# A hybrid attention layer in two-part fp32r: feature-major products as three 256-column matmuls into one shared bank

## The chip, the core and the metric

The kernel runs on one core of one Trainium2 chip. The metric is the device time of one execution in microseconds (us). The kernel before was run three times: 1160.6, 1161.08 and 1163.76 us, so its median is 1161.08 us. A profile of one further execution is what the argument is read from.

## The reference, cut to what matters

The input is 256 tokens of 2048 float32 features. One layer is computed:

```
h = rms_norm(x, attn_norm)
x = x + concat(norm(forgetting_attention), norm(stick_breaking_attention)) @ w_out   # both from h @ w_in
h = rms_norm(x, ffn_norm)
u = causal_conv3(h @ w_up) + conv_b          # depthwise, width 3 along the tokens, 11264 features
x = x + (silu(gate half of u) * value half of u) @ w_down                            # 5632 features
```

Everything is float32. Some 51 million weights are read once each; the profile counts 208.36 MB read from HBM.

## The kernel before, in words

**Two-part products.** TensorE's operands here are of the type fp32r, to which a float32 is rounded when it is written. To keep float32's accuracy, each operand a is split into `hi` = a rounded to fp32r and `lo` = a - `hi`, and a product sums three parts: hi·hi, hi·lo and lo·hi. `weights` (lines 202 to 215) brings 128 x 2048 weights (a piece: one DMA of 1024 KB into `w_raw`, three buffers), rounds them on ScalarE (ACT, line 210, `w_hi`, two buffers) and subtracts on VectorE (DVE, line 211, `w_lo`, two buffers). There are 204 such pieces. The activations are split once and stay: `hT[:, k]` is feature tile k, transposed, as [128 features, 2 parts, 256 tokens].

**Token-major products** (`token_major`, lines 220 to 240) hold 128 tokens of activations in the array (a load of 128 x 128, LDWEIGHTS) and stream 512 (in three column groups 344) columns of weights past them: three matmuls per feature tile and token tile, lines 235, 236 and 237, each with a load of its own. They serve most projections, the output projection and the down-projection.

**Feature-major products** (`feature_major`, lines 244 to 266) hold the weights in the array and stream the tokens, so that the result comes out as [features, tokens]. They serve the queries and keys of the stick-breaking attention (`sb_heads`, lines 474 to 483, eight calls) and the whole up-projection (`up_pair`, lines 599 to 606, 44 calls: 22 for gate tiles and 22 for value tiles). A call makes two tiles of 128 features from two pieces of weights. Per feature tile k and tile j of the two there are two matmuls: line 258 streams both parts of `hT[:, k]`, 512 columns, past `hi`, so that hi·hi lands in columns 0 to 255 of the tile's own PSUM bank and hi·lo in columns 256 to 511; line 262 streams 256 columns past `lo` and adds to the second half. With 16 feature tiles, 2 tiles j and 52 calls there are 1664 such pairs. The two halves of a bank are added afterwards: in `convolved` (lines 580 to 597) by an ACT copy of one half (line 586) and a DVE add (line 587), then a DVE product with the tokens' factor `R` (line 588), one ACT and two DVE operations of the convolution (lines 590 and 594), for each tile of 256 columns. `sb_heads` does the like in lines 480 to 482. The gate (lines 613 to 620) is a silu on ACT, a DVE product, and the split of the result into `g`, tile by tile.

**PSUM.** Eight banks: four of the pool `psa` (tag "acc"), and two each of the tags "s" and "t" of `psb`. A feature-major call takes two banks; in the up-projection every third call takes the two of tag "s".

**Order.** Every engine takes its instructions in one written order. The tile framework makes that order by priority; the weights' DMA, rounding and subtraction are given a priority 200 steps ahead of their place in the program (`AHEAD`), so that they stand between the convolution's instructions on ACT and DVE. The attention heads are generators, of which one step each is issued after a piece (`step`). The feed-forward runs in three parts of 16, 16 and 12 of the 44 gate tiles (`FFN_PARTS`): 32, 32 and 24 pieces of up-projection, each part followed by its share of the down-projection (16, 16 and 12 pieces).

Of the kernel before, what the change touches and what calls it, by code (L numbers as in the profile page):

```python
# [28 lines left out]

# Columns of the constant array.  # L30
C_ID, C_TRI, C_ONE = (P * i for i in range(3))
# [12 lines left out]
def hybrid_layer(  # L44
# [36 lines left out]

# [1 line left out]
    NC2 = 2 * NFT  # L83
# [48 lines left out]

# [1 line left out]
    pcol = const.tile([P, 50], F32, name="pcol")  # L134
# [12 lines left out]
    def transposed_split(k, g):  # L147
        """Feature tiles k and k + 1 of the tokens' rows, transposed, times g, in two parts."""
        ps = psb.tile([P, 2, S], F32, name="ps_x", tag="t")
        for j in range(2):  # L150
            for t in range(NT):
                nc.tensor.transpose(  # L152
                    ps[:, j, t * P : (t + 1) * P], xt[t][:, (k + j) * P : (k + j + 1) * P], ident
                )
        for j in range(2):
            i = k + j
            act.activation(hT[:, i, 0, :], ps[:, j, :], AF.Identity, scale=g[:, i : i + 1])
            dve.scalar_tensor_tensor(
                hT[:, i, 1, :], ps[:, j, :], g[:, i : i + 1], f32(hT[:, i, 0, :]),
                op0=ALU.mult, op1=ALU.subtract,  # L160
            )

    def sums_of_squares(ss, c):
        """Of 512 columns of each token tile."""
        for t in range(NT):
            junk = tmp.tile([P, 512], F32, name="junk", tag="raw", bufs=4)
            act.activation(junk, xt[t][:, c * 512 : (c + 1) * 512], AF.Square, accum_out=ss[:, t, c : c + 1])

    def token_factors(ss, n):
        """1 / rms of each token: per partition, and in every partition."""  # L170
        rstd = const.tile([P, NT], F32, name=f"rstd{n}")
        ssum = small.tile([P, NT], F32, name="ssum", tag="ssum")
        dve.tensor_reduce(ssum, ss, axis=AX.X, op=ALU.add)
        rsqrt(rstd, ssum, 1.0 / D, NT)
        dg = []
        for t in range(NT):
            dg.append(small.tile([P, P], F32, name="dg", tag="dg", bufs=2))
            dve.tensor_scalar(dg[t], ident, rstd[:, t : t + 1], None, op0=ALU.mult)
        return rstd, dg
# [8 lines left out]

# [1 line left out]
    waiting = deque()  # L190
# [9 lines left out]

# [1 line left out]
    def weights(src, a, b):  # L202
# [17 lines left out]
    def token_major(lhs, w, k0, nk, c0, cols, pieces=None, before=None):  # L220
        """[tokens, cols] = lhs.T @ w[k0:k0+nk, c0:c0+cols] for both token tiles."""
        acc = [psa.tile([P, 512], F32, name=f"acc{t}", tag="acc") for t in range(NT)]
# [21 lines left out]
    def feature_major(w, c0, spare):  # L244
        """Two tiles of features, each [features, tokens] in two summands."""
        nonlocal n_acc
        acc = []
        for j in range(2):
            pool, tag = (psa, "acc") if n_acc % 3 or not spare else (psb, "s")
            acc.append(pool.tile([P, 512], F32, name="pu", tag=tag))  # L250
        n_acc += 1
        for kh in range(2):
            hi, lo = weights(rows_of(w, 8 * kh, 8, c0, 2 * P), 8, 2 * P)
            for i in range(8):
                k = 8 * kh + i
                for j in range(2):
                    fs = slice(j * P, (j + 1) * P)
                    nc.tensor.matmul(  # L258
                        acc[j], hi[:, i, fs], hT[:, k].rearrange("p a b -> p (a b)"),
                        start=k == 0, stop=False,  # L260
                    )
                    nc.tensor.matmul(  # L262
                        acc[j][:, S:], lo[:, i, fs], hT[:, k, 0, :], start=False, stop=k == KT - 1
                    )
            step()
        return acc

    with ExitStack() as actx:
# [9 lines left out]
        def to_heads(dst, rows, t, scale):  # L278
            """Four heads' [tokens, dims] to [dims, tokens], times scale."""
            ps = psb.tile([P, 4, P], F32, name="ps_h", tag="t")  # L280
# [4 lines left out]
        def fox_rows(acc, dst, g):  # L285
            """Queries or keys of four heads: normalised, then transposed."""
            rows = []
# [19 lines left out]

        # The last four heads come when the projections are through with hT, and are used up
        # before its last rows are written again.
        oT = [at.tile([P, 2, S], F32R, name=f"oT{h}") for h in range(2 * NH - 4)]  # L310
# [3 lines left out]
        def attended(po, h, g, group):  # L314
            """Output of a head, [dims, tokens]: times its norm's weight in two parts, and its squares."""
            o = oT[group * NH + h]
# [10 lines left out]

# [1 line left out]
        # The first columns of weights are taken as x arrives.  # L329
        def opening(k, n):  # L330
# [52 lines left out]
        def gates():  # L383
            # log_sigmoid(y) = min(y, 0) - ln(1 + exp(-|y|))
            la = tmp.tile([P, NT, NH], F32, name="la", tag="la")
# [7 lines left out]
            yield  # L393
            # Cumulative log gates, the head h of row r*8+h, over the tokens.
            pc = psb.tile([P, 512], F32, name="pc", tag="t")
# [71 lines left out]

# [1 line left out]
        B0 = 3 * WF + NH  # L469
# [4 lines left out]
        def sb_heads(c0, scale, name):  # L474
            dst = heads_tile(name)
            for i in range(0, 4, 2):
                acc = feature_major(wi, c0 + i * P, False)
                for j in range(2):
                    t2 = tmp.tile([P, S], F32, name="t2", tag="t1", bufs=3)
                    act.copy(t2, acc[j][:, S:])  # L480
                    dve.tensor_tensor(t2, acc[j][:, :S], t2, op=ALU.add)
                    dve.tensor_tensor(dst[:, i + j, :], t2, scale, op=ALU.mult)
            return dst

        def sb_head(h, qT, kT, v):
# [8 lines left out]
            mm(z1, identR, maskS, start=False, stop=True)  # L494
            # softplus(z) = max(z, 0) + ln(1 + exp(-|z|))
            e = tmp.tile([P, 3 * P], F32, name="e", tag="pr")
# [8 lines left out]
            yield  # L505
            # z - sum of softplus over the keys from s on: the exponent of the weights.
            for i in range(2):
# [22 lines left out]

# [1 line left out]
        ss2 = const.tile([P, NT, 4], F32, name="ss2")  # L532
# [38 lines left out]

# [1 line left out]
    ff = ctx.enter_context(tc.tile_pool(name="ff", bufs=2))  # L573
    nu = 6
    up = [ff.tile([P, 2 + S], F32, name=f"up{i}") for i in range(nu)]
    for u in up:
        dve.memset(u[:, 0:2], 0.0)
    n_up = 0

    def convolved(ps, f):  # L580
        """Feature tile f after the up-projection, its token factor and its convolution."""
        nonlocal n_up
        u = up[n_up % nu]
        n_up += 1
        t2 = ff.tile([P, S], F32, name="t2", tag="t2", bufs=3)
        act.copy(t2, ps[:, S:])  # L586
        dve.tensor_tensor(t2, ps[:, :S], t2, op=ALU.add)  # L587
        dve.tensor_tensor(u[:, 2:], t2, R, op=ALU.mult)  # L588
        a = ff.tile([P, S], F32, name="cv", tag="cv", bufs=6)
        act.activation(  # L590
            a, u[:, 2:], AF.Identity, scale=ccol[:, 2, f : f + 1], bias=ccol[:, 3, f : f + 1]
        )
        for w in range(2):
            dve.scalar_tensor_tensor(  # L594
                a, u[:, w : w + S], ccol[:, w, f : f + 1], a, op0=ALU.mult, op1=ALU.add
            )
        return a

    def up_pair(f0):
        """Two feature tiles."""  # L600
        nonlocal R
        acc = feature_major(wu, f0 * P, True)
        if R is None:
            R = in_every_partition(dg2, 2)
            convolution_parameters()
        return [convolved(acc[j], f0 + j) for j in range(2)]

    gT = {}
    for n_part, (f_lo, f_hi) in enumerate(FFN_PARTS):
        for f in range(f_lo, f_hi, 2):  # L610
            gate = up_pair(f)
            val = up_pair(NFT + f)
            for j in range(2):
                sg = ff.tile([P, S], F32, name="sg", tag="sg")
                act.activation(sg, gate[j], AF.Silu)
                dve.tensor_tensor(sg, sg, val[j], op=ALU.mult)
                g2 = ff.tile([P, 2, S], F32R, name="g2", tag="g2", bufs=24)
                act.copy(g2[:, 0, :], sg)
                dve.tensor_tensor(g2[:, 1, :], sg, f32(g2[:, 0, :]), op=ALU.subtract)  # L619
                gT[f + j] = g2  # L620
        for c in range(4):
# [63 lines left out]
```

## Time and profile before

| | |
|---|---|
| three runs, median (lowest to highest) | 1161.08 us (1160.6 to 1163.76) |
| span of the profiled execution, first to last instruction | 1158.9 us |
| what lies around the span (median less span; the profile gives no other time of its own execution) | 2.2 us |
| TensorE matmul busy, records | 1147.0 us, 6002 |
| TensorE weight loads busy, records | 980.7 us, 6002 |
| DVE busy / ACT busy | 732.1 us (63%) / 559.1 us (48%) |
| DMA | 211.40 MB, mean 182 GB/s |

Times are counted from the first instruction of the execution. Engines: PE is TensorE's matmul, PEld its weight load, DVE VectorE, ACT ScalarE, SPq the queue that issues the DMAs. A line such as "L258 PE MATMUL pu<-hT,w_hi 128*128 128x512 f32 x1664 | 586.0, 397 | 0.0" reads: line 258 of the kernel, engine, operation, output from inputs, size of the loaded weights and of the result, number of instructions | busy time in us, mean ns of one | idle time of the engine just before them. Matmuls are pipelined, so a matmul's own duration overlaps with the next one's. A line of the timeline begins with the start and the duration in us.

### The profile page before, as it was taken

To read this page: it belongs to the slowest core of one execution; us is meant where nothing else is said; L and a number is where in the kernel's file an instruction comes from. 1 tells how busy PE (TensorE), PEld (TensorE's weight loads), DVE (VectorE), ACT (ScalarE), POOL (GpSimd) and SP (SyncE) were. 2 spreads that over 40 slices of the span, in tenths; PEclk is the share of its full clock that TensorE was granted. 3 is DMA by queue.
4 is the path that set the end of the run, shared out by engine and by line. 5 is a ranking of instruction groups with operands and counts; after the bars stand their busy time and mean duration, and the time that the engine had idled before them with its cause. 6 is when DMAs were issued, how large, how long until landed. Compare 5 with 4: busy or idle time off the path is not lost.

```text
span 1158.9 us, 14648 instructions
## 1 busy us (share of the span) xinstructions
PE 1147.0 (99%) x6002; PEld 980.7 (85%) x6002; DVE 732.1 (63%) x960; ACT 559.1 (48%) x716; POOL 0.2 (0%) x4
## 2 busy tenths in 40 slices
PE   7999999999999999999999999999999999999998
PEld 5998888888888888888888888888888888888886
DVE  4646656556465667777774547777775456777753
ACT  4644444445564555555553335555554334555531
POOL 0000000000000000000000000000000000000000
PEclk9999999999999999999999999999999999999999
DMA  6666545554444555555556555655556655555662
GB/s 226 212 219 204 179 149 181 158 171 150 159 158 151 182 170 194 182 182 183 183 189 199 191 182 183 196 194 190 182 185 198 197 183 182 183 188 184 192 231 76
DMA packets 162540, 211.40 MB, mean 182 GB/s; under 512 B 3736, under 2 KB 117546, under 8 KB 162474
## 3 DMA queue, kind: packets, MB, share of 16 engines
q1 hardware_dynamic: 162474, 210.47, 56.5%
q8 instruction: 47, 0.77, 0.3%
q14 instruction: 19, 0.16, 0.0%
HBM read 208.36 MB, written 2.10 MB: 182 GB/s over the span
## 4 chain that ended last, share of the span: by engine, by line
PE 97%; DVE 1%; ACT 1%; DMA 0%; issue 0%; SPq 0%
PE pu L258 33%; PE pu L262 17%; PE acc L235 14%; PE acc L237 14%; PE acc L236 14%; DVE w_lo L211 1%; ACT w_hi L210 1%; PE ps_x L152 1%; DMA x<-in_x_dram 0%; PE ps_h L282 0%; PE ps_z L491 0%; PE ps_s L423 0%; PE ps_o L517 0%; PE ps_o L450 0%; PE ps_p L444 0%
## 5 line engine op out<-in xcount | busy, mean ns | idle before, releaser
L211 DVE TENSOR_TENSOR w_lo<-w_raw,w_hi 128x2048 fp32r<-128x2048 f32 (+2 forms) x204 | 450.7, 2210 | 341.1 <-ACT w_hi L210 340.8
L258 PE MATMUL pu<-hT,w_hi 128*128 128x512 f32 x1664 | 586.0, 397 | 0.0
L210 ACT CAST w_hi<-w_raw 128x2048 fp32r<-128x2048 f32 (+2 forms) x204 | 375.7, 1842 | 368.1 <-PE acc L237 164.7
L262 PE MATMUL pu<-hT,w_lo 128*128 128x256 f32 x1664 | 466.6, 281 | 0.1
L258 PEld LDWEIGHTS pu<-hT,w_hi 128*128 128x128 f32 x1664 | 312.1, 188 | 73.7
L262 PEld LDWEIGHTS pu<-hT,w_lo 128*128 128x128 f32 x1664 | 314.3, 189 | 0.7 <-DVE w_lo L211 0.5
L237 PE MATMUL acc<-w_hi,g 128*128 128x512 f32 x352 | 139.0, 395 | 0.0
L235 PE MATMUL acc<-w_hi,g 128*128 128x512 f32 x352 | 138.9, 395 | 0.0
L236 PE MATMUL acc<-w_lo,g 128*128 128x512 f32 x352 | 138.9, 395 | 0.0
L235 PE MATMUL acc<-w_hi,hT 128*128 128x512 f32 (+1 forms) x320 | 119.8, 376 | 0.0
L236 PE MATMUL acc<-w_lo,hT 128*128 128x512 f32 (+1 forms) x320 | 119.1, 372 | 0.1
L237 PE MATMUL acc<-w_hi,hT 128*128 128x512 f32 (+1 forms) x320 | 118.9, 372 | 0.0
L594 DVE SCALAR_TENSOR_TENSOR cv<-up,ccol,cv 128x256 f32<-128x256 f32 x176 | 84.3, 479 | 1.6 <-ACT cv L590 0.7
L237 PEld LDWEIGHTS acc<-w_hi,g 128*128 128x128 f32 x352 | 66.3, 188 | 15.7 <-DVE g L619 0.2
L235 PEld LDWEIGHTS acc<-w_hi,g 128*128 128x128 f32 x352 | 66.3, 188 | 15.5
L236 PEld LDWEIGHTS acc<-w_lo,g 128*128 128x128 f32 x352 | 66.3, 188 | 15.4
L236 PEld LDWEIGHTS acc<-w_lo,hT 128*128 128x128 f32 x320 | 60.5, 189 | 9.0 <-DVE w_lo L211 0.9
L237 PEld LDWEIGHTS acc<-w_hi,hT 128*128 128x128 f32 x320 | 60.6, 189 | 8.7
L235 PEld LDWEIGHTS acc<-w_hi,hT 128*128 128x128 f32 x320 | 60.5, 190 | 8.2
L586 ACT COPY t<-pu 128x256 f32<-128x256 f32 x88 | 31.5, 360 | 58.8 <-PE pu L262 58.8
L590 ACT ACTIVATE cv<-up,ccol 128x256 f32<-128x256 f32 x88 | 52.6, 597 | 7.9 <-DVE up L588 5.6
L587 DVE TENSOR_TENSOR t<-pu,t 128x256 f32<-128x256 f32 x88 | 36.8, 420 | 21.9 <-ACT t L586 21.9
(148 smaller groups left out, 648.3 us busy)
## 6 DMA issues: line engine op xcount, KB each, us to landing
w_raw<-in_w_up_dram SPq DMA_DIRECT2D x88, 1024.0 KB, 5.1
w_raw<-in_w_down_dram SPq DMA_DIRECT2D x44, 1024.0 KB, 5.3
w_raw<-in_w_in_dram SPq DMA_DIRECT2D x36, 1024.0 KB, 5.2
w_raw<-in_w_out_dram SPq DMA_DIRECT2D x16, 1024.0 KB, 5.1
w_raw<-in_w_in_dram SPq DMA_DIRECT2D x12, 688.0 KB, 5.1
w_raw<-in_w_in_dram SPq DMA_DIRECT2D x8, 512.0 KB, 5.2
out_dram<-x SPq DMA_DIRECT2D x8, 256.0 KB, 5.3
x<-in_x_dram SPq DMA_DIRECT2D x3, 512.0 KB, 6.1
```

The lines of the kernel that those rows point to most:

```text
L152: nc.tensor.transpose(ps[:, j, t * P : (t + 1) * P], xt[t][:, (k + j) * P : (k + j + 1) * P], ident)
L210: act.copy(hi[:, :n], raw[:, :n])
L211: dve.tensor_tensor(lo[:, :n], raw[:, :n], f32(hi[:, :n]), op=ALU.subtract)
L235: nc.tensor.matmul(o, lhi, hi[:, i, :], start=first, stop=False)
L236: nc.tensor.matmul(o, lhi, lo[:, i, :], start=False, stop=False)
L237: nc.tensor.matmul(o, llo, hi[:, i, :], start=False, stop=last)
L258: nc.tensor.matmul(acc[j], hi[:, i, fs], hT[:, k].rearrange("p a b -> p (a b)"), start=k == 0, stop=False,)
L262: nc.tensor.matmul(acc[j][:, S:], lo[:, i, fs], hT[:, k, 0, :], start=False, stop=k == KT - 1)
L586: act.copy(t2, ps[:, S:])
L587: dve.tensor_tensor(t2, ps[:, :S], t2, op=ALU.add)
L590: act.activation(a, u[:, 2:], AF.Identity, scale=ccol[:, 2, f : f + 1], bias=ccol[:, 3, f : f + 1])
L594: dve.scalar_tensor_tensor(a, u[:, w : w + S], ccol[:, w, f : f + 1], a, op0=ALU.mult, op1=ALU.add)
```

## The change

`feature_major` now issues three matmuls of 256 columns each for a feature tile k and tile j: (`hi`, part 0), (`hi`, part 1) and (`lo`, part 0), all adding to the same 256 columns. The two tiles j share one bank, as the two halves of a [128, 2, 256] accumulator; only the very first matmul of the call clears. There are no two halves to be added any more, so the ACT copy and the DVE add go, and what follows works on both tiles at once: the product with `R` (or the scale of the queries and keys), the silu, the gate's product and its split run on 512 columns. The convolution's three operations stay per tile. The buffers are regrouped: four `up` buffers of two tiles for six of one, four `cv` of two for six of one, twelve `g2` of two tiles for 24 of one. The diff, without comments that it drops:

```diff
-        acc = []
-        for j in range(2):
-            pool, tag = (psa, "acc") if n_acc % 3 or not spare else (psb, "s")
-            acc.append(pool.tile([P, 512], F32, name="pu", tag=tag))
+        pool, tag = (psa, "acc") if n_acc % 3 or not spare else (psb, "s")
+        acc = pool.tile([P, 2, S], F32, name="pu", tag=tag)
...
-                    nc.tensor.matmul(
-                        acc[j], hi[:, i, fs], hT[:, k].rearrange("p a b -> p (a b)"),
-                        start=k == 0, stop=False,
-                    )
-                    nc.tensor.matmul(
-                        acc[j][:, S:], lo[:, i, fs], hT[:, k, 0, :], start=False, stop=k == KT - 1
-                    )
+                    for n, (a, b) in enumerate(((hi, 0), (hi, 1), (lo, 0))):
+                        nc.tensor.matmul(
+                            acc[:, j, :], a[:, i, fs], hT[:, k, b, :],
+                            start=k + j + n == 0, stop=k == KT - 1 and n == 2,
+                            skip_group_check=True,
+                        )
...
-                for j in range(2):
-                    t2 = tmp.tile([P, S], F32, name="t2", tag="t1", bufs=3)
-                    act.copy(t2, acc[j][:, S:])
-                    dve.tensor_tensor(t2, acc[j][:, :S], t2, op=ALU.add)
-                    dve.tensor_tensor(dst[:, i + j, :], t2, scale, op=ALU.mult)
+                dve.tensor_tensor(
+                    dst[:, i : i + 2, :], acc, scale.unsqueeze(1).to_broadcast([P, 2, S]), op=ALU.mult
+                )
...
-        t2 = ff.tile([P, S], F32, name="t2", tag="t2", bufs=3)
-        act.copy(t2, ps[:, S:])
-        dve.tensor_tensor(t2, ps[:, :S], t2, op=ALU.add)
-        dve.tensor_tensor(u[:, 2:], t2, R, op=ALU.mult)
-        a = ff.tile([P, S], F32, name="cv", tag="cv", bufs=6)
...
+        dve.tensor_tensor(u[:, :, 2:], ps, R.unsqueeze(1).to_broadcast([P, 2, S]), op=ALU.mult)
+        a = ff.tile([P, 2, S], F32, name="cv", tag="cv", bufs=4)
+        for j in range(2):
...
-            for j in range(2):
-                sg = ff.tile([P, S], F32, name="sg", tag="sg")
-                act.activation(sg, gate[j], AF.Silu)
-                dve.tensor_tensor(sg, sg, val[j], op=ALU.mult)
-                g2 = ff.tile([P, 2, S], F32R, name="g2", tag="g2", bufs=24)
-                act.copy(g2[:, 0, :], sg)
-                dve.tensor_tensor(g2[:, 1, :], sg, f32(g2[:, 0, :]), op=ALU.subtract)
-                gT[f + j] = g2
+            act.activation(gate, gate, AF.Silu)
+            dve.tensor_tensor(gate, gate, val, op=ALU.mult)
+            g2 = ff.tile([P, 2, 2, S], F32R, name="g2", tag="g2", bufs=12)
+            act.copy(g2[:, 0], gate)
+            dve.tensor_tensor(g2[:, 1], gate, f32(g2[:, 0]), op=ALU.subtract)
+            for j in range(2):
+                gT[f + j] = g2[:, :, j, :]
```

More of the change, by code (lines that the diff above doesn't have):

```diff
@@ L573, in hybrid_layer, with convolved @@
     ff = ctx.enter_context(tc.tile_pool(name="ff", bufs=2))
-    nu = 6
-    up = [ff.tile([P, 2 + S], F32, name=f"up{i}") for i in range(nu)]
+    nu = 4
+    up = [ff.tile([P, 2, 2 + S], F32, name=f"up{i}") for i in range(nu)]
     for u in up:
-        dve.memset(u[:, 0:2], 0.0)
+        dve.memset(u[:, :, 0:2], 0.0)
     n_up = 0
-    def convolved(ps, f):
+    def convolved(ps, f0):
         nonlocal n_up
@@ L584, in convolved @@
         n_up += 1
-        t2 = ff.tile([P, S], F32, name="t2", tag="t2", bufs=3)
-        act.copy(t2, ps[:, S:])
-        dve.tensor_tensor(t2, ps[:, :S], t2, op=ALU.add)
-        dve.tensor_tensor(u[:, 2:], t2, R, op=ALU.mult)
-        a = ff.tile([P, S], F32, name="cv", tag="cv", bufs=6)
[L590 to L595, printed above, removed]
-            )
+        dve.tensor_tensor(u[:, :, 2:], ps, R.unsqueeze(1).to_broadcast([P, 2, S]), op=ALU.mult)
+        a = ff.tile([P, 2, S], F32, name="cv", tag="cv", bufs=4)
+        for j in range(2):
+            f = f0 + j
+            act.activation(
+                a[:, j, :], u[:, j, 2:], AF.Identity,
+                scale=ccol[:, 2, f : f + 1], bias=ccol[:, 3, f : f + 1],
+            )
+            for w in range(2):
+                dve.scalar_tensor_tensor(
+                    a[:, j, :], u[:, j, w : w + S], ccol[:, w, f : f + 1], a[:, j, :],
+                    op0=ALU.mult, op1=ALU.add,
+                )
         return a
@@ L605, in up_pair @@
             convolution_parameters()
-        return [convolved(acc[j], f0 + j) for j in range(2)]
+        return convolved(acc, f0)
     gT = {}
```

## The prediction

> **What bounds the kernel now.** I read the page first, then the weight loads' waits, then the timeline of TensorE, which has what the page lacks: the time from one matmul's start to the next.
>
> ```profile
> span 1158.9 us, 14648 instructions
> PE 1147.0 (99%) x6002; PEld 980.7 (85%) x6002; DVE 732.1 (63%) x960; ACT 559.1 (48%) x716; POOL 0.2 (0%) x4
> PEclk9999999999999999999999999999999999999999
> PE 97%; DVE 1%; ACT 1%; DMA 0%; issue 0%; SPq 0%
> L258 PE MATMUL pu<-hT,w_hi 128*128 128x512 f32 x1664 | 586.0, 397 | 0.0
> L262 PE MATMUL pu<-hT,w_lo 128*128 128x256 f32 x1664 | 466.6, 281 | 0.1
> ```
> ```profile
> PEld pu L262 <- DVE w_lo L211: 0.5, 1, 0.5
> ```
>
> TensorE is the bound: 97% of the chain that ended last is its own work, at a granted clock that never falls. In the feature-major products it waits for nobody: 0.0 and 0.1 us idle before 3328 matmuls, and one wait of 0.5 us before a weight load. There is no stall to win back, so the change is worth what it does to TensorE's pace. The means of one (397 and 281 ns) aren't that pace, since neighbours overlap. The pace is the distance of the starts, first in the middle third of the up-projection, then in its first third:
>
> ```profile
> 699.67 0.39 PE L258 MATMUL pu<-hT,w_hi 128*128 128x512 f32 x1
> 699.90 0.28 PE L262 MATMUL pu<-hT,w_lo 128*128 128x256 f32 x1
> 700.01 0.39 PE L258 MATMUL pu<-hT,w_hi 128*128 128x512 f32 x1
> 700.24 0.28 PE L262 MATMUL pu<-hT,w_lo 128*128 128x256 f32 x1
> 700.36 0.39 PE L258 MATMUL pu<-hT,w_hi 128*128 128x512 f32 x1
> ...
> 703.83 0.39 PE L258 MATMUL pu<-hT,w_hi 128*128 128x512 f32 x1
> ```
> ```profile
> 479.61 0.40 PE L258 MATMUL pu<-hT,w_hi 128*128 128x512 f32 x1
> 479.85 0.28 PE L262 MATMUL pu<-hT,w_lo 128*128 128x256 f32 x1
> 479.97 0.40 PE L258 MATMUL pu<-hT,w_hi 128*128 128x512 f32 x1
> ...
> 489.86 0.40 PE L258 MATMUL pu<-hT,w_hi 128*128 128x512 f32 x1
> ```
> ```profile
> 480.00:580.00 100.00, 100.00 (x569) 1.00 0.57 182
> 720.00:820.00 100.00, 100.00 (x579) 1.00 0.59 191
> 960.00:1060.00 100.00, 100.00 (x568) 1.00 0.57 183
> ```
>
> From 699.67 to 703.83 stand 12 pairs (512 columns, then 256): 4.16 / 12 = 0.3467 us a pair. From 479.61 to 489.86 stand 29: 10.25 / 29 = 0.3534 us. The same code thus runs in two rhythms. The stretches of 100 us (matmuls in brackets) show that each keeps to its part: 579 matmuls in the middle part, 569 and 568 in the first and last. I give the quick rhythm to the middle part's 32 x 16 = 512 pairs, and the slow one to the other 1664 - 512 = 1152, those of the stick-breaking attention with them, where other matmuls stand between.
>
> **The change part by part.** *The matmuls.* The columns streamed stay: 512 + 256 = 3 x 256. Each pair becomes three matmuls, so 1664 matmuls are added, and 1664 weight loads with them. That a load comes with each matmul, even where the weights in the array already are the wanted ones, shows in lines 235 and 236, which use the same weights one after the other:
>
> ```profile
> L235 PEld LDWEIGHTS acc<-w_hi,g 128*128 128x128 f32 x352 | 66.3, 188 | 15.5
> L236 PEld LDWEIGHTS acc<-w_lo,g 128*128 128x128 f32 x352 | 66.3, 188 | 15.4
> ```
>
> So the whole question is what a matmul of 256 columns costs among others of 256. The trace has none, so I bound it by its neighbours: a run of 512-column matmuls in the attention, a run of 344-column ones, and a run of 512 in the down-projection.
>
> ```profile
> 105.79 0.39 PE L235 MATMUL acc<-w_hi,hT 128*128 128x512 f32 x1
> ...
> 111.91 0.39 PE L235 MATMUL acc<-w_hi,hT 128*128 128x512 f32 x1
> ```
> ```profile
> 51.25 0.32 PE L237 MATMUL acc<-w_hi,hT 128*128 128x344 f32 x1
> ...
> 58.96 0.32 PE L235 MATMUL acc<-w_hi,hT 128*128 128x344 f32 x1
> ```
> ```profile
> 620.03 0.39 PE L237 MATMUL acc<-w_hi,g 128*128 128x512 f32 x1
> ...
> 625.60 0.40 PE L237 MATMUL acc<-w_hi,g 128*128 128x512 f32 x1
> ```
>
> 27 steps of 512 take 6.12 us, 0.2267 each; 49 steps of 344 take 7.71 us, 0.1573 each. Their difference is 0.0694 us for 168 columns, 0.413 ns a column. A step of 512 is then 0.2115 for its columns and 0.0152 that doesn't depend on them. A step of 256 is 256 x 0.413 ns + 0.0152 = 0.1209 us. The pair says the same: 0.3467 - 0.2267 = 0.1200 us is left for its 256 columns. In the slow rhythm the run of 512 takes 5.57 / 24 = 0.2321, and 0.3534 - 0.2321 = 0.1213 is left. Three methods agree within 1%, so I take the price of a third matmul to be the fixed part that each has beside its columns:
>
> - middle part: 512 x (3 x 0.1200 - 0.3467) = 512 x 0.0133 = 6.8 us
> - the rest: 1152 x (3 x 0.1213 - 0.3534) = 1152 x 0.0105 = 12.1 us
>
> Together 18.9 us lost. The bounds of the 256-column step are wide. Above: it can't cost more than the 344-column step, which has the same two instructions and more columns: 0.1573, or 3 x 0.1573 = 0.472 a triple, about 200 us lost. Below: its columns alone, 0.1057, or 0.317 a triple, about 57 us won. The value taken lies by the pair itself, the nearest row. I judge the step by sums because the single starts disagree with them: line 262 is followed 0.11 or 0.12 us later, line 258 0.23 or 0.24. Read straight, the 256-column step is 0.1167, and that makes a rival.
>
> The Trainium skill, page "TensorE: Matmul & The Clock Gate", section "Back-to-back issue gap", would put the fixed part of a warm matmul at 2.5 ns beside N / 2.4 ns for N columns; by this, as an estimate, a pair takes 0.325 us, and the third matmul costs 1664 x 0.0025 = 4.2 us. The trace's 0.3467 doesn't agree. The same page, section "LDWEIGHTS (loading the stationary operand)", has a load of 128 columns take 128 / 1.2 = 107 ns, which would leave it hidden.
>
> *The weight loads.* They stand beside the matmuls as long as one takes no longer than the matmul before it. The recorded 188 ns overlap too; the nearest rows for the distance of two are those of a run of 256- and 128-column matmuls in a stick-breaking head, where the loads follow one another:
>
> ```profile
> 290.77 0.19 PEld L509 LDWEIGHTS ps_z<-sps,masksR 128*128 128x128 f32 x1
> 290.88 0.19 PEld L510 LDWEIGHTS ps_z<-sps,masksR 128*128 128x128 f32 x1
> 291.00 0.19 PEld L511 LDWEIGHTS ps_z<-sps,masksR 128*128 128x128 f32 x1
> ```
>
> 0.11 and 0.12 us: under the 0.12 of a step, but just. Today every second load has 0.23 us. That cover goes, and each 1 ns by which a step exceeds its price costs 3 x 1664 x 0.001 = 5.0 us.
>
> *What ACT and DVE lose and gain.* Rows for the feed-forward:
>
> ```profile
> L586 ACT COPY t<-pu 128x256 f32<-128x256 f32 x88 | 31.5, 360 | 58.8 <-PE pu L262 58.8
> L587 DVE TENSOR_TENSOR t<-pu,t 128x256 f32<-128x256 f32 x88 | 36.8, 420 | 21.9 <-ACT t L586 21.9
> L588 DVE TENSOR_TENSOR up<-t,R 128x256 f32<-128x256 f32 x88 | 37.0, 423 | 1.4
> L625 DVE TENSOR_TENSOR x<-acc,x 128x512 f32<-128x512 f32 x24 | 16.5, 691 | 13.3 <-PE acc L237 13.2
> ```
>
> 88 copies (31.5 us) and 88 adds (36.8 us) go; 88 products (37.0 us) become 44 of 512 columns, by line 625's 691 ns 30.4 us. ACT gets about 32 us less and DVE 43, and the eight calls in the attention a little more. None of it is on the path, since TensorE doesn't wait, so I count nothing. What matters is whether the weights still come in time:
>
> ```profile
> 702.04 1.90 ACT L210 CAST w_hi<-w_raw 128x2048 fp32r<-128x2048 f32 x1
> 703.96 2.29 DVE L211 TENSOR_TENSOR w_lo<-w_raw,w_hi 128x2048 fp32r<-128x2048 f32 x1 [1.95 <-ACT w_hi L210]
> ...
> 707.53 1.89 ACT L210 CAST w_hi<-w_raw 128x2048 fp32r<-128x2048 f32 x1
> ```
>
> Rounding (1.90) and subtraction (2.29) follow one another, 4.2 us of the 16 x 0.3467 = 5.55 us that TensorE spends on a piece; with two buffers that leaves about 1.3 us. The longest new instruction that can stand in front is one of 512 columns, 0.69 us by line 625, where it was 0.42: 0.3 us off the reserve on each of the two engines, while the longer piece gives back 0.2. I count nothing; if both are late at once, a piece loses some tenths. Half the PSUM banks go free as well, but TensorE waited for none. The added instructions don't weigh on DMA: 1024 KB a piece stay.
>
> The sum: 1161.1 + 18.9 = **1180 us**. It is made on the profiled execution: its span would go from 1158.9 to about 1177.8, and the 2.2 us between that span and the runs' median stay.
>
> **The rivals.** *No price for the third matmul (same).* The starts read straight give the 256-column step 0.1167 in both rhythms (0.3467 - 0.23; 0.3534 - 0.2367, the mean of 0.24, 0.24 and 0.23 as the starts round). Then 3 x 0.1167 = 0.350: 512 x 0.0033 = 1.7 us lost, 1152 x 0.0034 = 3.9 won, 1159 us in all. For it: these are the starts of real 256-column steps with a load beside them. Against: what a 256 seems to save there, its 512 pays (0.23 against 0.2267). The page's 2.5 ns would also end near here, at 1165.
>
> *Loads in series (slower still).* If a load can begin only when the matmul before it starts, and the next matmul only when it is done, the step is the load's 0.12 and a handover. With 0.125, the triple is 0.375: 512 x 0.0283 + 1152 x 0.0216 = 39.4 us, **1200 us**. For it: the loads' starts keep to the matmuls' starts, and 0.12 stood beside a 256-column matmul. Against: 0.11 stood there too. The same would show if TensorE's instructions were issued no faster than the 344-column run needs, two in 0.157 us.
>
> *The slow rhythm goes (faster).* The rhythm belongs to the order of long and short steps. If a stream of equal steps has none, and the third matmul costs nothing, the 1152 slow pairs go to 0.3467: 1152 x 0.0067 = 7.7 us won, **1153 us**. It decides from a 256-column step under 0.1171, a third of the mean pair (512 x 0.3467 + 1152 x 0.3534) / 1664 = 0.3513. For it: the middle part shows that the code can run so, and steps of 0.11 occur. Against: the fixed part in the runs of equal columns.
>
> **How the numbers follow.** My forecast, the fixed part paid 1664 times (1172 to 1188 us): 0.53. No price: 0.21. Loads in series: 0.14. Slow rhythm gone: 0.12. A measurement of this kernel can tell about 0.3%, 3.5 us, from no change. Faster by more than that: the last rival and a little of the first, 0.16. Within it: 0.15. Slower: 0.69. The range goes from 1156 us, which takes in all of the same-case and leaves most of the faster one out, to 1200 us, which cuts the series case in half.
>
> **What would show it.** Some 4992 matmuls at one line, 7666 in all, with as many loads. The starts of 256-column matmuls in the up-projection should stand 0.120 to 0.121 us apart, a piece 5.76 to 5.82 us (48 steps). No idle before them but tenths. Wrong would be: 0.117 or less; 0.125 or more; a wait of the loads for `w_lo` of several us in all; or a down-projection whose own step moves away from 0.232.

## The result, and the profile after

The changed kernel takes 1168.42 us (median of six runs, 1168.09 to 1169.79); the kernel before, on the same chip, 1160.84 us. The ratio is 1.0055, 95% interval 1.0039 to 1.0070: 6.4 us slower by the ratio, where 18.9 were forecast. The profiled execution took 1168.34 us with a span of 1166.5 us, 7.6 more than before.

The page of the changed kernel first:

```profile
span 1166.5 us, 17603 instructions
PE 1154.8 (99%) x7666; PEld 1069.2 (92%) x7666; DVE 685.7 (59%) x758; ACT 527.1 (45%) x568; POOL 0.2 (0%) x4
PE 96%; DVE 2%; ACT 1%; DMA 0%; issue 0%; SPq 0%
L258 PE MATMUL pu<-hT,w_hi 128*128 128x256 f32 x3328 | 601.1, 283 | 0.0
L258 PE MATMUL pu<-hT,w_lo 128*128 128x256 f32 x1664 | 471.0, 283 | 0.1
L581 DVE TENSOR_TENSOR up<-pu,R 128x512 f32<-128x512 f32 x44 | 30.4, 692 | 57.5 <-PE pu L258 57.5
```

TensorE is still the bound and still waits for nothing in these products. There are 7666 matmuls and as many weight loads, 1664 more of each. DVE has 46 us less work and ACT 32, and it shows nowhere in the time.

Now the starts, in the first third of the up-projection and in the down-projection behind it, where the prediction showed the same places of before:

```profile
479.98 0.28 PE L258 MATMUL pu<-hT,w_lo 128*128 128x256 f32 x1
480.10 0.40 PE L258 MATMUL pu<-hT,w_hi 128*128 128x256 f32 x2
480.34 0.28 PE L258 MATMUL pu<-hT,w_lo 128*128 128x256 f32 x1
...
485.74 0.28 PE L258 MATMUL pu<-hT,w_lo 128*128 128x256 f32 x1
...
619.73 0.39 PE L235 MATMUL acc<-w_hi,g 128*128 128x512 f32 x1
...
625.17 0.39 PE L235 MATMUL acc<-w_hi,g 128*128 128x512 f32 x1
```

From 479.98 to 485.74 stand 16 triples: 5.76 / 16 = 0.3600 us, or 0.1200 a step. From 619.73 to 625.17 stand 24 steps of 512: 5.44 / 24 = 0.2267, where it was 0.2321 before. The stretches count the matmuls (in brackets) in the three parts of the up-projection and, in the last row, in the first down-projection; the second fence is the same stretch of the kernel before:

```profile
480.00:580.00 100.00, 100.00 (x836) 1.00 0.58 187
720.00:820.00 100.00, 100.00 (x835) 1.00 0.56 181
960.00:1060.00 100.00, 100.00 (x836) 1.00 0.57 186
610.00:670.00 60.00, 60.00 (x266) 1.00 0.59 193
```
```profile
610.00:670.00 60.00, 60.00 (x260) 1.00 0.57 185
```

The up-projection has one rhythm in all its parts now, and the down-projection, whose matmuls the change doesn't touch, is quicker: 266 in 60 us for 260. Laid out by pieces of weights (mean time from a piece's first load to the next one's):

| pieces | before, us | after, us | difference in all |
|---|---|---|---|
| 16 feature-major, stick-breaking attention | 6.459 | 6.594 | +2.2 |
| 32, up-projection, first part | 5.719 | 5.829 | +3.5 |
| 32, second part | 5.550 | 5.763 | +6.8 |
| 24, third part | 5.658 | 5.764 | +2.5 |
| 16 + 16 + 12, down-projection | 5.570, 5.569, 5.580 | 5.435, 5.435, 5.433 | -6.1 |
| first 8, as x arrives | 3.440 | 3.312 | -1.0 |

Together 7.9, where the spans differ by 7.6 us. The opening's 1.0 isn't the change's doing: in two kernels below whose opening is that of before (the rest alone, and the pad in the kernel before), the first eight pieces took 3.28 and 3.46 us each. So two questions: why the added matmuls cost 15.0 and not 18.9, and where the 6.1 us of the down-projection come from.

### The profile page after: what moved, and what is told of

The parts are those of the page before. It is cut to its first block, busy times and chain, and to the rows that moved or that the text cites. A ratio compares the mean times of both kernels' runs of the same rounds, so it can differ in the third digit from the quotient of the medians.

```text
span 1166.5 us, 17603 instructions
## 1 busy us (share of the span) xinstructions
PE 1154.8 (99%) x7666; PEld 1069.2 (92%) x7666; DVE 685.7 (59%) x758; ACT 527.1 (45%) x568; POOL 0.2 (0%) x4
## 4 chain that ended last, share of the span: by engine, by line
PE 96%; DVE 2%; ACT 1%; DMA 0%; issue 0%; SPq 0%
PE pu L258 51%; PE acc L235 14%; PE acc L236 14%; PE acc L237 14%; DVE w_lo L211 1%; ACT w_hi L210 1%; PE ps_x L152 1%; DMA x<-in_x_dram 0%; PE ps_h L280 0%; PE ps_z L487 0%; PE ps_o L448 0%; PE ps_s L421 0%; PE ps_o L513 0%; PE ps_p L442 0%; PE ps_z L505 0%
## 5 line engine op out<-in xcount | busy, mean ns | idle before, releaser
L258 PE MATMUL pu<-hT,w_hi 128*128 128x256 f32 x3328 | 601.1, 283 | 0.0
L258 PEld LDWEIGHTS pu<-hT,w_hi 128*128 128x128 f32 x3328 | 519.1, 192 | 0.2
L258 PEld LDWEIGHTS pu<-hT,w_lo 128*128 128x128 f32 x1664 | 319.3, 192 | 0.3 <-DVE w_lo L211 0.3
L235 PE MATMUL acc<-w_hi,g 128*128 128x512 f32 x352 | 137.0, 389 | 0.0
L237 PE MATMUL acc<-w_hi,g 128*128 128x512 f32 x352 | 136.9, 389 | 0.0
L590 DVE SCALAR_TENSOR_TENSOR cv<-up,ccol,cv 128x256 f32<-128x256 f32 x176 | 73.5, 479 | 0.7 <-ACT cv L585 0.7
L581 DVE TENSOR_TENSOR up<-pu,R 128x512 f32<-128x512 f32 x44 | 30.4, 692 | 57.5 <-PE pu L258 57.5
L585 ACT ACTIVATE cv<-up,ccol 128x256 f32<-128x256 f32 x88 | 48.0, 592 | 2.7 <-DVE ccol L566 2.7
L235 PE MATMUL acc<-w_hi,oT 128*128 128x512 f32 x96 | 38.1, 397 | 0.0
```

The source lines that it names most:

```text
L235: nc.tensor.matmul(o, lhi, hi[:, i, :], start=first, stop=False)
L237: nc.tensor.matmul(o, llo, hi[:, i, :], start=False, stop=last)
L258: nc.tensor.matmul(acc[:, j, :], a[:, i, fs], hT[:, k, b, :], start=k + j + n == 0, stop=k == KT - 1 and n == 2, skip_group_check=True,)
L581: dve.tensor_tensor(u[:, :, 2:], ps, R.unsqueeze(1).to_broadcast([P, 2, S]), op=ALU.mult)
L585: act.activation(a[:, j, :], u[:, j, 2:], AF.Identity, scale=ccol[:, 2, f : f + 1], bias=ccol[:, 3, f : f + 1],)
L590: dve.scalar_tensor_tensor(a[:, j, :], u[:, j, w : w + S], ccol[:, w, f : f + 1], a[:, j, :], op0=ALU.mult, op1=ALU.add,)
```

## The experiments

Theory A: the slow steps of the down-projection are a state that the mixed 512/256 stream carries in. Theory B: something else in the change, the grouping of the `g` tiles or the lighter ACT and DVE, made them quick. Each kernel below was compared with the kernel before on the same chip, which took 1160.69, 1162.82 and 1160.59 us in the three groups of four.

**The split alone.** In the kernel before, line 258's matmul becomes two of 256 columns; banks, copies, adds and buffers stay.

```diff
-  matmul(acc[j], hi[:, i, fs], hT[:, k] as 512 columns)
+  matmul(acc[j][:, :S], hi[:, i, fs], hT[:, k, 0, :])
+  matmul(acc[j][:, S:], hi[:, i, fs], hT[:, k, 1, :])
   matmul(acc[j][:, S:], lo[:, i, fs], hT[:, k, 0, :])
```

> The kernel before with its feature-major pair made three matmuls of 256 columns, into the same two banks, halves added as before; buffers, g tiles and ACT/DVE operations as before. Theory A (history): the slow rhythm of 0.2321 us a step in the down-projection is a state that TensorE's stream carries in from the mixed 512/256 pairs, and equal matmuls don't make it. Then the up-projection's step is 0.120, the down-projection's 0.2267, and the time lies about 15 us above and 6 us below the kernel before: 1169 us. Theory B (place): the new grouping of the g tiles, or the lighter ACT and DVE, made the down-projection quick. Then its step stays 0.232 here and the time is about 1175 us.

Measured: 1175.02 us, 1.0121 (1.0106 to 1.0137). A stretch of the up-projection and the one in the first down-projection:

```profile
480.00:580.00 100.00, 100.00 (x836) 1.00 0.57 185
610.00:670.00 60.00, 60.00 (x260) 1.00 0.57 193
```

The up-projection took 5.76 us a piece in all three parts (0.120 a step), just as in the changed kernel, and the down-projection stayed slow. Theory A fails.

**The rest alone.** The changed kernel with the old pairs, two banks, copies and adds.

> The matmul pairs of 512 and 256 columns as before, in two banks, with the copies and adds of the halves; but the feed-forward's up, cv and g buffers grouped by two tiles, and the product with R, the silu, the gate's product and the split on 512 columns, as in the changed kernel (the attention's queries and keys as before). Theory A (history): pairs of 0.3467 to 0.3534, down-projection at 0.232, 1161 us. Theory B (place): the down-projection goes to 0.2267, 1056 matmuls by 0.0054 us, so 1155 us.

Measured: 1155.42 us, 0.9949 (0.9937 to 0.9961).

```profile
480.00:580.00 100.00, 100.00 (x578) 1.00 0.58 190
720.00:820.00 100.00, 100.00 (x568) 1.00 0.56 184
960.00:1060.00 100.00, 100.00 (x568) 1.00 0.56 183
610.00:670.00 60.00, 60.00 (x267) 1.00 0.59 195
```

The quick down-projection comes with the regrouping, though no matmul is split. The rows hold a second thing: the quick rhythm of the pairs (578 in 100 us) is now in the first part, where in the kernel before it was in the second.

**A clean entry.** Only the last feature-major call ahead of each down-projection is split as above; the added argument marks it.

```diff
-            val = up_pair(NFT + f)
+            val = up_pair(NFT + f, f == f_hi - 2)
```

> The kernel before, with only the last feature-major call ahead of each of the three down-projections made of three matmuls of 256 columns (96 of the 1664 pairs, by 0.0133 us at most 1.3 us more). Theory A (history): the down-projection is entered from equal matmuls and runs at 0.2267 from its first piece on, 5.7 us less, so 1156 us; what the second and third part of the up-projection do when entered from a quick down-projection is open, 0.3467 or 0.3534. Theory B (place): the g tiles are those of before, the down-projection stays at 0.232, 1162 us.

Measured: 1163.87 us, 1.0016 (1.0005 to 1.0027).

```profile
610.00:670.00 60.00, 60.00 (x260) 1.00 0.58 192
```

260 again, entered from equal steps. That is the second blow to Theory A.

**Like matmuls together.** Both 512-column matmuls of a feature tile, then both of 256.

```diff
-  for j in range(2): matmul 512 (hi, j); matmul 256 (lo, j)
+  for j in range(2): matmul 512 (hi, j)
+  for j in range(2): matmul 256 (lo, j)
```

> The kernel before with the order of its four matmuls of a feature tile changed: both of 512 columns first, then both of 256 (before: 512, 256, 512, 256). Sizes and counts stay. Theory A in its narrow form (long next to short upsets the stream, like next to like settles it): all parts at 2 x 0.2267 + 2 x 0.1200 = 0.6933 us for the four, that is 0.3467 a pair, and the down-projection at 0.2267: 1152 pairs by 0.0067 and 1056 matmuls by 0.0054 less, 1147 us. If any mixture upsets it, or Theory B holds: some parts at 0.3534, the down-projection at 0.232, 1161 us.

Measured: 1155.71 us, 0.9955 (0.9943 to 0.9967).

```profile
480.00:580.00 100.00, 100.00 (x577) 1.00 0.58 190
720.00:820.00 100.00, 100.00 (x576) 1.00 0.58 190
960.00:1060.00 100.00, 100.00 (x576) 1.00 0.58 190
610.00:670.00 60.00, 60.00 (x260) 1.00 0.58 191
```

Half of what the narrow form of Theory A says came. The slow rhythm of the pairs (568 in 100 us) is gone from all parts: 5.573 us a piece or 0.3483 a pair, nearly the quick one's 0.3467. The down-projection stays slow. The rhythm of the pairs and the pace of the down-projection are two things.

**Where the buffers lie.** In the compiled programs the split-alone kernel's `g` tiles start, like those of before, at byte 158688 of a partition, 224 modulo 256; those of the changed kernel at 159584 and of the rest alone at 163680, both 96 modulo 256. The weights streamed past them start at 96 in all. So the next edit, in the kernel before, is one unused tile ahead of the feed-forward's buffers.

```diff
     ff = ctx.enter_context(tc.tile_pool(name="ff", bufs=2))
+    dve.memset(ff.tile([P, 32], F32, name="pad", bufs=1), 0.0)
```

> The kernel before with one unused tile of 128 bytes a partition ahead of the feed-forward's buffers, so that all of them, the 24 g tiles among them, start 128 bytes higher: modulo 256 at 96 where they started at 224. Nothing else is changed. Theory B1 (address): the down-projection's slow rhythm comes from where its loaded operand g starts; the kernels with 224 (before and the one with the split alone) had 0.232, those with 96 (the changed one and the one with the rest alone) 0.2267. Then 0.2267 here, 1155 us. Theory B2 (layout: the two parts of a g tile 2048 bytes apart instead of 1024, two tiles side by side) or B3 (fewer, wider operations on ACT and DVE): 0.232, 1161 us.

Measured: 1157.49 us, 0.9952 (0.9939 to 0.9964).

The same tile in the changed kernel:

> The changed kernel with the same unused tile of 128 bytes, which moves its g tiles from 96 to 224 modulo 256. B1 (address): the down-projection falls to 0.232 a step, 1056 matmuls by 0.0054 us are 5.7 us more, 1174 us. B2 and B3: 0.2267, 1168.4 us.

Measured: 1174.69 us, 1.0102 (1.0089 to 1.0116).

The same tile in the version with like matmuls together:

> The kernel before with both matmuls of 512 columns ahead of both of 256, which alone took 1155.7 us with pairs of 0.3483 in all three parts and the down-projection at 0.232, and with the unused tile of 128 bytes. B1 (address): the two gains add, 1155.7 - 5.7 = 1150 us. B2 and B3: 1155.7 us.

Measured: 1149.48 us, 0.9888 (0.9873 to 0.9903), the fastest version here. The first down-projection in the kernel before with the pad, in the changed kernel with the pad, and in the version with like matmuls together and the pad:

```profile
610.00:670.00 60.00, 60.00 (x267) 1.00 0.59 194
```
```profile
610.00:670.00 60.00, 60.00 (x260) 1.00 0.56 188
```
```profile
610.00:670.00 60.00, 60.00 (x266) 1.00 0.59 195
```

128 bytes make the down-projection of the old kernel quick and that of the changed one slow. That settles B1, the address, against the layout and the load of ACT and DVE. (The tile moves all the feed-forward's buffers; of these TensorE reads `g` alone.)

**Which address.** The same pad at the very start of the kernel moves weights, `hT` and `g` alike.

> The kernel before with an unused tile of 128 bytes at the very start, so that the weights, hT, the attention's outputs and the g tiles all move by 128: weights and hT from 96 to 224 modulo 256, g from 224 to 96. B1 absolute (what counts is where the loaded operand itself starts): the token-major products of the attention part, 0.2267 until now, fall to 0.232 (960 matmuls, some 5 us more), the down-projection rises to 0.2267 (5.7 us less); about 1160 us, if the pairs stay. B1 relative (what counts is where the loaded operand lies against the streamed one): loaded and streamed operand still differ by 128 modulo 256 in the down-projection alone, so that stays at 0.232 and the attention at 0.2267; 1161 us. B2, B3: as relative.

Measured: 1163.07 us, 1.0001 (0.9989 to 1.0013).

```profile
480.00:580.00 100.00, 100.00 (x568) 1.00 0.57 183
720.00:820.00 100.00, 100.00 (x568) 1.00 0.57 185
960.00:1060.00 100.00, 100.00 (x568) 1.00 0.59 190
610.00:670.00 60.00, 60.00 (x260) 1.00 0.58 188
105.18 0.39 PE L236 MATMUL acc<-w_hi,hT 128*128 128x512 f32 x1
...
111.30 0.39 PE L236 MATMUL acc<-w_hi,hT 128*128 128x512 f32 x1
```

The down-projection stays slow with `g` at 96, since the weights are at 224 now. The attention's steps of 512 (27 from 105.18 to 111.30) keep their 6.12 / 27 = 0.2267, though `hT` is at 224. What counts is the difference between the loaded and the streamed operand. All three parts of the pairs fell into the slow rhythm here.

Two more places of `g`, in the version with like matmuls together (pads of 16 and of 8 elements):

> As the version with like matmuls together and the pad, but the pad is 64 bytes: g tiles start at 32 modulo 256, the weights streamed past them at 96, so that the two differ by 64 (0 took 0.2267 a step, 128 took 0.232). If any difference that isn't a multiple of 256 upsets the down-projection: 0.232, 1155 us. If only 128 does: 0.2267, 1149.5 us. If the fixed part of a step is itself a matter of place: below 0.2267 and below 1149.

Measured: 1151.62 us, 0.9921 (0.9909 to 0.9934).

> The same with a pad of 32 bytes: g tiles start at 0 modulo 256, 96 below the weights. Any difference upsets it: 0.232, 1155 us. Only 128 does: 0.2267, 1149.5 us. Fixed part a matter of place: below 0.2267.

Measured: 1156.25 us, 0.9962 (0.9950 to 0.9975).

The first down-projection, with `g` 64 bytes below the weights modulo 256 and then 96 below:

```profile
610.00:670.00 60.00, 60.00 (x264) 1.00 0.59 192
```
```profile
610.00:670.00 60.00, 60.00 (x259) 1.00 0.58 191
```

By the median piece, over 24 steps: a difference of 0 modulo 256 gives 0.2267, of 64 bytes 5.493 / 24 = 0.2289, of 128 bytes 0.2322, of 96 bytes 5.600 / 24 = 0.2333. Each of the three differences tried costs something, but not one fixed amount, as the expectations had it, and none is below 0.2267.

**The other products.** `hT` moved by 128 bytes against the weights in the changed kernel; the attention's outputs and `g` put back.

> The changed kernel with hT (and x) moved up by 128 bytes, and the attention's outputs and the g tiles padded back to 96 modulo 256. Weights and hT now differ by 128 in the products from hT: token-major in the attention, where hT is loaded and weights are streamed, and feature-major, where weights are loaded and hT is streamed. If the difference by 128 of loaded against streamed operand is the rule whichever is which: the token-major 512-column steps of the attention go to 0.232 (and the 344-column ones rise too), the 256-column steps of the up-projection above 0.120, and the down-projection stays at 0.2267; 672 x 0.0054 = 3.6 us more and, if 4992 steps rise by a proportional 2%, some 12 more, 1180 to 1185 us. If equal steps are proof against it, as in no run so far: up-projection at 0.120, about 1172 us. If the rule is one of the g tiles alone: 1168.4 us.

Measured: 1168.99 us, 1.0074 (1.0060 to 1.0087) against the kernel before, level with the changed kernel's 1.0055 (1.0039 to 1.0070).

```profile
96.77 0.40 PE L238 MATMUL acc<-w_hi,hT 128*128 128x512 f32 x1
...
105.14 0.39 PE L238 MATMUL acc<-w_hi,hT 128*128 128x512 f32 x1
```
```profile
480.00:580.00 100.00, 100.00 (x845) 1.00 0.58 190
720.00:820.00 100.00, 100.00 (x836) 1.00 0.56 181
```

The attention's 36 steps from 96.77 to 105.14 took 8.37 / 36 = 0.2325 (0.2267 before): the rule holds where `hT` is loaded. The 256-column steps of the feature-major products didn't rise at all: for equal steps of 256, loaded from the weights, the place by 128 bytes costs nothing. That is the second case of the expectation, but for one thing. In the first part they fell, to 5.695 / 48 = 0.1186 (845 in 100 us), while the second and third part kept 0.1200. So equal steps too can run in two rhythms, each for a whole part, and 0.1200 isn't the least that such a step takes. What picks it is open.

**Why a step of 256 takes 0.120.** In the changed kernel, the product of `lo` is cut once more, into two of 128 columns, which stand between the two products of `hi`.

```diff
-  matmul 256 (hi, part 0); matmul 256 (hi, part 1); matmul 256 (lo, part 0)
+  matmul 256 (hi, part 0)
+  matmul 128 (lo, part 0, tokens 0 to 127); matmul 128 (lo, part 0, tokens 128 to 255)
+  matmul 256 (hi, part 1)
```

> The changed kernel with the product of lo cut once more, into two matmuls of 128 columns with the same weights: four matmuls and four loads for a feature tile and tile of two. It asks why 256 columns take 0.120. If a step is its columns and a fixed part of 0.0133: 2 x 0.120 + 2 x 0.0667 = 0.3733 where three take 0.360, 16 x 0.3733 = 5.97 us a piece, 1664 x 0.0133 = 22 us more, about 1190 us. If weight loads in series set the step, at 0.11 to 0.12 each: 0.44 to 0.48, 7.1 to 7.7 us a piece, 140 to 200 us more, 1310 to 1370 us.

Measured, in one run: 1339.59 us. The weight loads, two to a row:

```profile
540.08 0.31 PEld L261 LDWEIGHTS pu<-hT,w_lo 128*128 128x128 f32 x2
540.31 0.30 PEld L266 LDWEIGHTS pu<-hT,w_hi 128*128 128x128 f32 x2
540.54 0.31 PEld L261 LDWEIGHTS pu<-hT,w_lo 128*128 128x128 f32 x2
```

Two loads every 0.23 us, a piece 7.41 us for 64 of them: 0.116 each. Here the columns don't set the pace: the loads stand nearly evenly, 0.109 to 0.121 us one behind the other, beside matmuls of 128 and of 256 columns alike. That the load itself is the limit fits best; a limit on how fast TensorE's instructions are issued, which the prediction names, would look the same and isn't ruled out. A step of 256 at 0.120 thus stands about where its columns with the fixed part (0.1209 by the prediction's sum) and its load meet. Which of them sets it isn't separated by these runs.

## Why the prediction was right or wrong, point by point

- **TensorE bounds, and the work of ACT and DVE counts for nothing: right.** They lost 32 and 46 us of it, and the up-projection takes the 5.76 us a piece that it takes with the split alone, where they lost none; the weight loads' waits in the up-projection stayed at tenths.
- **A 256-column step at 0.1200: right in size**, by sums and not by single starts. It is 0.1200 in every part, in the changed kernel and with the split alone. For the middle part 6.8 us were forecast and 6.8 came. The reason given, a fixed part that each matmul has beside its columns, isn't shown: by it the kernel with matmuls of 128 columns would take about 1190 us, and it took 1339.59. That it gave the right price at 256 columns may in part be luck. The rival without a price (0.1167) falls: the third matmul costs 0.3600 - 0.3467 = 13.3 ns beside the quick pair. With it falls, for this stream, the 2.5 ns of fixed cost that the Trainium skill, page "TensorE: Matmul & The Clock Gate", section "Back-to-back issue gap", gives for an isolated warm matmul.
- **12.1 us for the other 1152 pairs: too much**, 8.2 came (2.2 + 3.5 + 2.5). The step that failed is "In the slow rhythm ... 0.1213 is left". It took the down-projection's 0.2321 for the 512 columns of a slow pair, but that step has its length from the place of `g`: with like matmuls together the slow rhythm was gone and the down-projection as slow as ever. And it carried the slow rhythm into the triples, which take 0.3600 in all parts of the changed kernel. So the slow pair pays 0.3600 - 0.3534 = 6.6 ns, not 10.5. The rival that the slow rhythm goes was right in that and wrong in the price, since the third matmul is paid as well.
- **No term for the regrouped buffers: this is where most of the error lies.** With "I count nothing" I priced the instructions on ACT and DVE at nothing, which held, but I didn't ask where the buffers come to lie. The regrouping moved the `g` tiles 896 bytes up, and with that from a difference of 128 bytes to none against the weights: 1056 matmuls by 0.2321 - 0.2267, some 5.7 us, 6.1 by the pieces. The prediction named a down-projection that leaves 0.232 as a sign of error, and gave it no term.
- **Loads in series at 0.125: wrong here**, but near: with matmuls of 128 columns among those of 256, loads 0.116 apart most likely set the pace.

18.9 - 3.9 (the rhythm) - 6.1 (the place) - 1.0 (the opening) is 7.9, against 7.6 measured by the spans. With the `g` tiles left in their old place, the split alone costs 1.0121, 14 us.

Open: what picks the rhythm of the 512/256 pairs. In five profiles with such pairs throughout or nearly so, the quick one was in the second part (before), the first (rest alone, clean entry, pad) or in none (everything shifted). A part of 512 pairs by 0.0067 is 3.4 us, which would fit the spread of the kernel before (1159.5 to 1164.3 us), but no run shows that directly. The kernel with everything shifted ran from 1159.35 to 1164.01 us, one program at one set of addresses, so the program alone doesn't seem to decide it. Equal steps have shown a second rhythm in one profile, that with `hT` moved.

## What to carry to other kernels

Where TensorE is the bound, count matmuls as well as columns: cutting a 512-column matmul in two cost 7 to 13 ns each time here, and what it freed on other engines was hidden. A change of buffers moves addresses, so read the pace of stages that the change doesn't touch, and try a pad before crediting the edit. Take a step's price from a long run of starts, not from neighbours, and from a run whose operands lie as those of the step to be priced.

## What the runs showed of the hardware

- A token-major step of 512 fp32r columns took 0.2267 us when the loaded and the streamed operand start at the same byte modulo 256, and 0.2289, 0.2333 and 0.2322 at differences of 64, 96 and 128 bytes. The 128 bytes were tried both in the down-projection and in the attention, the others in the down-projection alone.
- An alternating stream of 512 and 256 columns ran at 0.3467 or at 0.3534 us a pair, each for a whole part; 512, 512, 256, 256 ran at 0.3483 in every part. Steps of 256 alone ran at 0.1200, but at 0.1186 for a whole part in the kernel with `hT` moved.
- Weight loads of 128 columns in series stood 0.109 to 0.121 us apart beside matmuls of 128 and 256 columns. The Trainium skill's 107 ns ("TensorE: Matmul & The Clock Gate", section "LDWEIGHTS (loading the stationary operand)") agrees with the shortest of them; the mean is 0.116.
- The two edits that came out of this, like matmuls together and 128 bytes of pad, made the kernel 1.1% faster (0.9888) with the same instructions but one.
